# Scores of the HGRN2 layer on four quarters of the array, with the samples' products beside them

## The chip, the core and the metric

The kernel runs on one core of a Trainium2 chip. A core has five engines that matter here, each with its own instruction stream: TensorE (PE; the profile shows its weight loads apart, as PEld), VectorE (DVE), ScalarE (ACT), GpSimd (POOL) and SyncE (SP), whose queue here issues all transfers. Matrix products land in PSUM, a memory of eight banks with 128 partitions; a bank holds 512 F32 values of each partition. The metric is the time of one execution on the device in microseconds, lower is better.

## The reference, cut to what matters

One step of a two-layer decoder trunk: 256 new prompt tokens and 8 single-token samples go through a Conformer convolution layer, a feed-forward layer with a causal convolution, an HGRN2 layer (gated linear recurrence, 16 heads of 128 x 128 state) and a second feed-forward layer. The change touches only the HGRN2 layer. Its core, for one head:

```python
def step(S, inp):
    qc, kc, vc, gc = inp
    G = jnp.cumsum(gc, axis=1)
    o_inter = jnp.einsum('bthk,bhkv->bthv', qc * jnp.exp(G), S)
    rel = jnp.where(mask[None, :, :, None, None], G[:, :, None] - G[:, None, :], -jnp.inf)
    decay = jnp.exp(rel)
    A = jnp.einsum('bthk,btshk,bshk->bths', qc, decay, kc)
    o_intra = jnp.einsum('bths,bshv->bthv', A, vc)
    ...
```

So the output of token t is a sum over the earlier tokens s of a score, which is the product of query t and key s in each of 128 channels, weighted by the decay between the two tokens in that channel, times the value of s. The samples are single tokens with a state of their own: their state decays, takes in the outer product of key and value, and is multiplied by the query.

## The kernel before, in words

All activations stay on the chip, with channels on the partitions and the 264 tokens (256 and 8) along the free axis. Weights are streamed in tiles of 128 output channels. `slot` (L183) does one such tile: 16 steps over the input channels, each of three products of 264 columns in a fast F32 form (L179 to L181, a high and a low part of weight and activation), so 48 products of a slot. The parts are made ahead by ACT (`split_hi`, L137) and DVE (`split_lo`, L149).

PE, ACT and DVE run in the order in which the program is written. `later(k, fn)` (L159) puts a step into the turn of the slot that comes k + 1 slots later; within a turn (`slot`, L196 to L204), after the slot's 48 products have been put on PE, come the steps marked `first`, the casts, the unmarked steps, the splits on DVE, and the steps marked `last`. SP's order is made by a planner, which follows the data and the buffers.

In the HGRN2 stage each head takes three slots: `hf` (forget gate), `hq` (query), `hi` (value). After the heads in `GATE_AFTER` (3, 4, 6, 7, 9, 10, 12, 13, 15) comes one slot `hg` (output gate) of an earlier head, and the seven remaining `hg` slots come at the end. The stage is followed by the output projection (`ho`), whose first tile is a plain F32 product (L176).

The scores are computed without exponents of long sums. `doubling` (L677) makes, for b = 1, 2, 4, ..., 128, pairs `R[b]` of queries and keys, already decayed to the border inside blocks of 2b tokens. The score of tokens t and s is right in that level b in which s lies in the first and t in the second half of the same block of 2b; for t = s it is the plain product. So each level gives a matrix of which a mask keeps a part, and the masked levels are summed. `scores` (L741) does that inside blocks of 64 tokens: for each of the seven entries of `LV` (0, 1, 2, 4, 8, 16, 32) and each of the four blocks of 64 there is one product of 64 x 64 (L750), two blocks on the lower and two on the upper half of the array's columns, into `pl`, two banks. Then come level 128 (L753, 128 x 128) and level 64 (L756, two products of 64 x 64, both on the lower half) into one bank `pa`, and two transposes that turn keys for the state (L759). All are plain F32. `flip` (L709) turns the values, just ahead of `scores` in the same turn.

`select` (L761), one turn later, copies the parts of `pa` out on ACT, multiplies `pl` with the mask (L769) and sums over the levels (L772) on DVE; `place` (L774) copies the result into `AT`, the matrix of weights, whose part above the blocks of 64 comes from level 64 (L766). `outputs` (L796) multiplies by the values.

For the samples, `decay` (L779) scales the state on ACT, `sample_state` (L788) adds the outer products on DVE and writes the state out (L794), and `sample_outputs` (L806) multiplies it with the queries: eight products with 32 columns of weights, four of them side by side on four quarters of the array's columns, into `pos` (L813). That is a step of its own at the end of a turn, two turns after `decay`. After the last head `sample_rows`, `sample_columns`, `sample_squares`, `sample_sum` and `sample_norm` (L872 to L895) normalise all samples at once, and `samples_gated` (L923) applies the gates.

Of the kernel before, what the change touches and what calls it, by code (L numbers as in the profile page):

```python
# [8 lines left out]
F32 = mybir.dt.float32  # L9
# [3 lines left out]
ALU = mybir.AluOpType  # L13
AX = mybir.AxisListType
# [3 lines left out]
P = 128  # L18
# [6 lines left out]
HEADS = 16  # L25
# [20 lines left out]
AHEAD = 2  # L46
LOADS = 4
TE = 17

GATE_AFTER = (3, 4, 6, 7, 9, 10, 12, 13, 15)  # L50
HGRN, _g = [], 0
# [9 lines left out]
def kernel(ctx: ExitStack, tc: tile.TileContext, a: dict):  # L61
# [4 lines left out]
    cp = ctx.enter_context(tc.tile_pool(name="cp", bufs=1))  # L66
    sp = ctx.enter_context(tc.tile_pool(name="sp", bufs=1))
    wp = ctx.enter_context(tc.tile_pool(name="wp", bufs=3))
    ps = ctx.enter_context(tc.tile_pool(name="ps", bufs=5, space=PSUM))

    def bank(name):
        return ps.tile([P, 512], F32, tag="pt", name=name)
# [541 lines left out]
    with ExitStack() as ph:  # L614
# [3 lines left out]
        rstd = st.y  # L618
        later(0, st.finish, last=True)

        mask = cst[:, P:].rearrange("p (o n) -> p o n", o=1).to_broadcast((P, 2, len(LV) * 64))
        AT = [h1.tile([P, 2, P], F32, tag=f"AT{i}", name=f"AT{i}") for i in range(2)]
        for t in AT:
            vec.memset(t[64:, :, :64], 0.0)
        gss = h1.tile([P, HEADS, NB], F32, tag="gss", name="gss")

        NG = P // 32
# [113 lines left out]
        def scores(h):  # L741
            d = heads[h]
            R, qk, K = d["R"], d["qk"], d["K"]
            pl = d["pl"] = ps.tile([P, 2, 512], F32, tag="pl", name=f"pl{h}", bufs=1)
            for l, b in enumerate(LV):
                for hf in range(2):
                    for i in range(2):
                        s = (2 * hf + i) * 64
                        key, query = (qk[:, 2, :], qk[:, 0, :]) if b == 0 else (R[b][:, 1, :], R[b][:, 0, :])
                        pe.matmul(pl[i * 64 : i * 64 + 64, hf, l * 64 : (l + 1) * 64], key[:, s : s + 64], query[:, s : s + 64],  # L750
                                  start=True, stop=True)
            pa = d["pa"] = bank(f"pa{h}")
            pe.matmul(pa[:, :P], R[128][:, 1, :P], R[128][:, 0, P:SEQ], start=True, stop=True)  # L753
            for hf in range(2):
                s = hf * P
                pe.matmul(pa[:64, P + hf * 64 : P + (hf + 1) * 64], R[64][:, 1, s : s + 64], R[64][:, 0, s + 64 : s + P],  # L756
                          start=True, stop=True)
            for i, k in enumerate((K, R[128][:, 1, P:SEQ])):
                pe.transpose(pa[:, (2 + i) * P : (3 + i) * P], k, ident)  # L759

        def select(h):  # L761
            d = heads[h]
            pa, pl, W = d.pop("pa"), d.pop("pl"), AT[h % 2]
            Kt = d["Kt"] = hp.tile([P, 2, P], F32, tag="Kt", name=f"Kt{h}", bufs=1)
            act.copy(Kt, pa[:, 2 * P :].rearrange("p (i k) -> p i k", i=2))
            act.copy(W[:64, :, 64:], pa[:64, P : 2 * P].rearrange("p (o t) -> p o t", o=2))  # L766
            A1 = d["A1"] = hp.tile([P, P], F32, tag="A1", name=f"A1_{h}", bufs=1)
            act.copy(A1, pa[:, :P])
            vec.tensor_tensor(out=pl[:, :, : len(LV) * 64], in0=pl[:, :, : len(LV) * 64], in1=mask, op=ALU.mult)  # L769
            lm = pl[:, :, : len(LV) * 64].rearrange("p o (l t) -> p o t l", t=64)  # L770
            wd = heads[h]["wd"] = hp.tile([P, 2, 64], F32, tag="wd", name=f"wd{h}", bufs=1)
            vec.tensor_reduce(out=wd, in_=lm, axis=AX.X, op=ALU.add)  # L772

        def place(h):  # L774
            for i in range(2):
                r = slice(i * 64, i * 64 + 64)
                act.copy(AT[h % 2][r, :, r], heads[h]["wd"][r])

        def decay(h):  # L779
            d = heads[h]  # L780
# [146 lines left out]
        for name, h in HGRN:  # L927
            pt, = slot([(name, h)], hl)
            if name == "hf":
                later(0, lambda h=h, pt=pt: forget(h, pt), first=h > 0)  # L930
            elif name == "hq":
                if h == 0:
                    later(0, turned, last=True)
                    later(1, windows, last=True)
                later(0, lambda h=h, pt=pt: query(h, pt), first=True)
                later(0, lambda h=h: doubling(h, 1, 4), last=True)
            elif name == "hi":
                later(0, lambda h=h, pt=pt: value(h, pt), first=True)
                later(0, lambda h=h: doubling(h, 4, SEQ))
                later(1, lambda h=h: flip(h), last=True)  # L940
                later(1, lambda h=h: scores(h), last=True)
                later(2, lambda h=h: rows(h), first=True)
                later(2, lambda h=h: select(h))
                later(2, lambda h=h: place(h), last=True)
                later(3, lambda h=h: decay(h))
                later(3, lambda h=h: outputs(h), last=True)
                later(4, lambda h=h: squares(h), first=True)
                later(4, lambda h=h: sample_state_and_norm(h))
                later(5, lambda h=h: sample_outputs(h), last=True)
                later(5, lambda h=h: normed(h))  # L950
                later(6, lambda h=h: flop(h), last=True)
                later(7, lambda h=h: columns(h), first=True)
                if h == HEADS - 1:
                    later(6, sample_rows, first=True)
                    later(6, sample_columns, last=True)
                    later(7, sample_squares, first=True)
                    later(7, sample_sum, last=True)
                    later(8, sample_norm, first=True)
                    later(8, lambda: samples_gated(0, HEADS - 2), last=True)
                    later(8, lambda: samples_gated(HEADS - 2, HEADS), last=True)  # L960
            else:
                later(0, lambda h=h, pt=pt: gates(h, pt), first=True)
                later(0, lambda h=h: gated(h))
# [15 lines left out]
    with ExitStack() as ph:  # L979
        yp = ph.enter_context(tc.tile_pool(name="yp", bufs=1))  # L980
        Q = D // 4
        y = [yp.tile([P, D], F32, tag=f"y{i}", name=f"y{i}") for i in range(2)]
        ys = yp.tile([P, KT, NB], F32, tag="ys", name="ys")
        turned = {}

        def turn_back(i, c, pt):
            turned[i, c] = pt
            for j in range(4):
                pe.transpose(pt[:, j * P : (j + 1) * P], x[4 * c + j][:, i * P : (i + 1) * P], ident)

        pl = ps.tile([P, 2, 512], F32, tag="pl", name="p_y", bufs=1)
        pt = ps.tile([P, 512], F32, tag="st", name="p_ss", bufs=1)
        for i in range(2):
            turn_back(i, 0, bank(f"p_y{i}_0"))

        for i in range(3):
            for src, first in (st.acc, True), (st.last, False):
                if i < 2:
                    pe.matmul(pt[:, i * P : i * P + 1], src[:, i * P : (i + 1) * P], ones[:, :1], start=first, stop=not first)
                else:  # L1000
                    pe.matmul(pt[:, SEQ:T], ones, src[:, SEQ:], start=first, stop=not first)
        for i in range(2):
            turn_back(i, 1, pl[:, i, :])
        steps, r = [], []
        for s, w in (pt[:, 0:SEQ:P], 2), (pt[:, SEQ:T], NB):
            v, t, z = (yp.tile([P, w], F32, tag=f"{name}{w}", name=f"final_{name}{w}") for name in "vtr")
            vec.tensor_scalar(out=v, in0=s, scalar1=1.0 / D, scalar2=EPS, op0=ALU.mult, op1=ALU.add)
            steps.append(rsqrt_steps(z, v, t))
            r.append(z)
        for _ in zip(*steps):  # L1010
            pass
        for c in range(2, 4):
            for i in range(2):
                turn_back(i, c, bank(f"p_y{i}_{c}"))
        for c in range(4):
            d = slice(c * Q, (c + 1) * Q)
            act.activation(y[0][:, d], turned[0, c], AF.Identity, scale=r[0][:, 0:1])
            vec.tensor_scalar(out=y[1][:, d], in0=turned[1, c], scalar1=r[0][:, 1:2], scalar2=None, op0=ALU.mult)
            if c == 1:
                vec.tensor_tensor(out=ys, in0=xall[:, :, SEQ:], in1=r[1].unsqueeze(1).to_broadcast((P, KT, NB)), op=ALU.mult)  # L1020
                nc.sync.dma_start(a["o_ys"], ys)
            for i in range(2):
                nc.sync.dma_start(a["o_y"][i * P : (i + 1) * P, d], y[i][:, d])
# [93 lines left out]
```

## Time and profile before

| what | us |
|---|---|
| median of three runs (2478.6 to 2479.64) | 2479.0 |
| the profiled execution | 2478.74 |
| its span, first to last instruction | 2477.0 |
| PE busy over the span | 2446.4 |
| DVE busy over the span | 1759.9 |
| ACT busy over the span | 1110.7 |
| HGRN2 stage with its end, from 1132 to 1594 | 462 |
| in it, busy: PE, DVE, ACT | 455.4, 371.6, 267.1 |

The first two lines are times of whole executions; everything below comes from the profile of one of them, so a sum made from the profile is set against 2478.74. An engine is busy while it has an instruction in work. Products are pipelined, so PE's busy time alone doesn't say how well the array is used; starts of successive products do. The granted clock of PE was 0.996 of full speed over the span.

### The profile page before, as it was taken

To read this page: it belongs to the slowest core of one execution; us is meant where nothing else is said; L and a number is where in the kernel's file an instruction comes from. 1 tells how busy PE (TensorE), PEld (TensorE's weight loads), DVE (VectorE), ACT (ScalarE), POOL (GpSimd) and SP (SyncE) were. 2 spreads that over 40 slices of the span, in tenths; PEclk is the share of its full clock that TensorE was granted. 3 is DMA by queue.
4 is the path that set the end of the run, shared out by engine and by line. 5 is a ranking of instruction groups with operands and counts; after the bars stand their busy time and mean duration, and the time that the engine had idled before them with its cause. 6 is when DMAs were issued, how large, how long until landed. Compare 5 with 4: busy or idle time off the path is not lost.

```text
span 2477.0 us, 46795 instructions
## 1 busy us (share of the span) xinstructions
PE 2446.4 (99%) x19878; PEld 2391.7 (97%) x19878; DVE 1759.9 (71%) x3087; ACT 1110.7 (45%) x1759; POOL 0.2 (0%) x4
## 2 busy tenths in 40 slices
PE   8999899999999999999999999899999999999998
PEld 7888899999999999999999999899999999999998
DVE  8999867766566567568887888657767657656655
ACT  1112645444344344345655665444444444435434
POOL 0000000000000000000000000000000000000000
PEclk9999999999999999999999999999999999999999
DMA  7444445554554554555655655455555455455453
GB/s 270 150 153 142 169 173 204 176 182 156 202 187 161 182 196 164 180 182 197 232 190 202 222 208 199 161 182 199 176 187 173 158 205 180 158 201 186 164 176 129
DMA packets 78129, 452.92 MB, mean 183 GB/s; under 512 B 8544, under 2 KB 13024, under 8 KB 39008
## 3 DMA queue, kind: packets, MB, share of 16 engines
q1 hardware_dynamic: 77920, 449.94, 51.6%
q8 instruction: 155, 2.54, 0.4%
q14 instruction: 54, 0.44, 0.0%
HBM read 436.31 MB, written 15.50 MB: 182 GB/s over the span
## 4 chain that ended last, share of the span: by engine, by line
PE 99%; DVE 1%; issue 0%; DMA 0%; ACT 0%; ACTq 0%; SPq 0%; DVEq 0%
PE p_up L181 14%; PE p_up L179 14%; PE p_up L180 14%; PE p_pw L176 10%; PE p_dn L181 7%; PE p_dn L180 7%; PE p_dn L179 7%; PE p_hi L179 1%; PE p_hg L179 1%; PE p_hf L179 1%; PE p_hq L179 1%; PE p_hf L181 1%; PE p_hg L181 1%; PE p_hq L181 1%; PE p_hi L181 1%; PE p_hi L180 1%
## 5 line engine op out<-in xcount | busy, mean ns | idle before, releaser
L179 PE MATMUL p_up<-h_ffn,wh_up 128*128 128x264 f32 x2816 | 801.1, 284 | 0.0
L181 PE MATMUL p_up<-h_ffn,wl_up 128*128 128x264 f32 x2816 | 800.7, 284 | 0.0
L180 PE MATMUL p_up<-l_ffn,wh_up 128*128 128x264 f32 x2816 | 797.5, 283 | 0.0
L149 DVE TENSOR_TENSOR wl_up<-w_up,wh_up 128x2048 fp32r<-128x2048 f32 x176 | 403.5, 2293 | 231.9 <-ACT wh_up L137 231.9
L137 ACT CAST wh_up<-w_up 128x2048 fp32r<-128x2048 f32 x176 | 335.9, 1909 | 505.9 <-PE p_up L180 446.8
L179 PEld LDWEIGHTS p_up<-h_ffn,wh_up 128*128 128x128 f32 x2816 | 530.1, 188 | 0.1
L181 PEld LDWEIGHTS p_up<-h_ffn,wl_up 128*128 128x128 f32 x2816 | 530.0, 188 | 0.0
L180 PEld LDWEIGHTS p_up<-l_ffn,wh_up 128*128 128x128 f32 x2816 | 529.6, 188 | 0.1
L181 PE MATMUL p_dn<-gh,wl_dn 128*128 128x264 f32 x1408 | 400.8, 285 | 0.0
L179 PE MATMUL p_dn<-gh,wh_dn 128*128 128x264 f32 x1408 | 400.3, 284 | 0.0
L180 PE MATMUL p_dn<-gl,wh_dn 128*128 128x264 f32 x1408 | 400.1, 284 | 0.0
L137 ACT CAST wh_dn<-w_dn 128x1408 fp32r<-128x1408 f32 x128 | 175.9, 1374 | 325.9 <-PE p_dn L180 243.8
L149 DVE TENSOR_TENSOR wl_dn<-w_dn,wh_dn 128x1408 fp32r<-128x1408 f32 x128 | 208.1, 1626 | 108.3 <-ACT wh_dn L137 108.3
L180 PEld LDWEIGHTS p_dn<-gl,wh_dn 128*128 128x128 f32 x1408 | 265.3, 188 | 0.0
L181 PEld LDWEIGHTS p_dn<-gh,wl_dn 128*128 128x128 f32 x1408 | 264.7, 188 | 0.0
L179 PEld LDWEIGHTS p_dn<-gh,wh_dn 128*128 128x128 f32 x1408 | 264.6, 188 | 0.0
L176 PE MATMUL p_pw<-xg,w_pw 128*128 128x264 f32 x960 | 213.9, 386 | 0.0
L176 PEld LDWEIGHTS p_pw<-xg,w_pw 128*128 128x128 f32 x960 | 182.4, 190 | 31.2
L567 DVE SCALAR_TENSOR_TENSOR C<-H,par,C 128x255 f32<-128x255 f32 x352 | 169.1, 480 | 6.3
L278 DVE TENSOR_TENSOR x<-x,p_dn 128x264 f32<-128x264 f32 x128 | 54.9, 429 | 111.9 <-PE p_dn L181 111.9
L561 DVE TENSOR_TENSOR H<-p_up,rstd_ffn 128x264 f32<-128x264 f32 x176 | 76.1, 432 | 78.3 <-PE p_up L181 78.3
L562 ACT ACTIVATE C<-H,par 128x264 f32<-128x264 f32 x176 | 105.5, 600 | 13.9 <-DVE H L561 13.9
(316 smaller groups left out, 4007.9 us busy)
## 6 DMA issues: line engine op xcount, KB each, us to landing
w_up<-in_up SPq DMA_DIRECT2D x176, 1024.0 KB
w_dn<-in_dn SPq DMA_DIRECT2D x128, 704.0 KB
w_pw<-in_pw SPq DMA_DIRECT2D x47, 1024.0 KB
w_hf<-in_hf SPq DMA_DIRECT2D x16, 1024.0 KB
w_hq<-in_hq SPq DMA_DIRECT2D x16, 1024.0 KB
w_hi<-in_hi SPq DMA_DIRECT2D x16, 1024.0 KB
w_hg<-in_hg SPq DMA_DIRECT2D x16, 1024.0 KB
w_ho<-in_ho SPq DMA_DIRECT2D x16, 1024.0 KB
```

What stands on the lines that cost most here:

```text
L137: act.copy(wh[:, :kk, :], raw[key][:, :kk, :])
L149: vec.tensor_tensor(out=wl[:, :kk, :], in0=raw.pop(key)[:, :kk, :], in1=wh.bitcast(F32)[:, :kk, :], op=ALU.subtract)
L176: pe.matmul(pt[:, :T], wh[:, k, :], full[k], start=(k == 0), stop=last)
L179: pe.matmul(pt[:, :T], wh[:, k, :], rh, start=(k == 0), stop=False)
L180: pe.matmul(pt[:, :T], wh[:, k, :], rl, start=False, stop=False)
L181: pe.matmul(pt[:, :T], wl[:, k, :], rh, start=False, stop=last)
L278: vec.tensor_tensor(out=x[n], in0=x[n], in1=pt[:, :T], op=ALU.add)
L561: vec.tensor_tensor(out=h, in0=pt[:, :T], in1=rstd, op=ALU.mult)
L562: act.activation(cc, h, AF.Identity, scale=wv[:, j, 2:3], bias=pcol("ffn_b", layer * 2 * FT + j))
L567: vec.scalar_tensor_tensor(out=cc[:, d:SEQ], in0=h[:, : SEQ - d], scalar=wv[:, j, 2 - d : 3 - d], in1=cc[:, d:SEQ], op0=ALU.mult, op1=ALU.add)
```

## The change

`scores` works in blocks of 32 tokens. For the levels 0 to 16 each of the eight blocks of 32 is one product of 32 x 32, on the quarter of the array's columns that belongs to its place in the 128 tokens. Level 32 is no longer masked: of each block of 64 only the rectangle of the first 32 keys and the second 32 queries is computed. Level 64 is cut into four products of 32 keys by 64 queries, one on each quarter. All these, and then the sample products of the head before (`sample_outputs(h - 1)`), stand in a row ahead of level 128. `pl` is one bank instead of two, and the pool of general banks grows from five to six.

`select` masks and sums six levels of 32 columns instead of seven of 64 (384 values of each partition instead of 896). Level 32 is copied straight from `pl` into `AT` by two copies, level 64 by two instead of one, and `place` makes four copies instead of two. `AT` is cleared whole at the start of the stage, and the mask is rearranged by two copies there.

The sample products of a head are no step of their own any more, apart from those of the last head, which stand one turn earlier than before; the steps that normalise the samples all move one turn up, and `sample_norm` is no longer at the head of its turn. At the kernel's end one of the transposed parts of the output takes a general bank, since `pl` has only one.

```diff
+B = 32
+NL = len(LV) - 1
...
-    ps = ctx.enter_context(tc.tile_pool(name="ps", bufs=5, space=PSUM))
+    ps = ctx.enter_context(tc.tile_pool(name="ps", bufs=6, space=PSUM))
...
-        mask = cst[:, P:].rearrange("p (o n) -> p o n", o=1).to_broadcast((P, 2, len(LV) * 64))
+        by_level = cst[:, P:].rearrange("p (l t) -> p l t", t=64)
+        for r in (B, 3 * B):
+            act.copy(by_level[r : r + B, :NL, :B], by_level[r : r + B, :NL, B:])
+        mask = by_level[:, :NL, :B].unsqueeze(1).to_broadcast((P, 2, NL, B))
...
-            vec.memset(t[64:, :, :64], 0.0)
+            vec.memset(t, 0.0)
...
-            pl = d["pl"] = ps.tile([P, 2, 512], F32, tag="pl", name=f"pl{h}", bufs=1)
+            pl = d["pl"] = ps.tile([P, 2, len(LV), B], F32, tag="pl", name=f"pl{h}", bufs=1)
+            pa = d["pa"] = bank(f"pa{h}")
             for l, b in enumerate(LV):
+                key, query = (qk[:, 2, :], qk[:, 0, :]) if b == 0 else (R[b][:, 1, :], R[b][:, 0, :])
                 for hf in range(2):
-                    for i in range(2):
-                        s = (2 * hf + i) * 64
-                        key, query = (qk[:, 2, :], qk[:, 0, :]) if b == 0 else (R[b][:, 1, :], R[b][:, 0, :])
-                        pe.matmul(pl[i * 64 : i * 64 + 64, hf, l * 64 : (l + 1) * 64], key[:, s : s + 64], query[:, s : s + 64],
-                                  start=True, stop=True)
-            pa = d["pa"] = bank(f"pa{h}")
+                    for i in range(0, P // B, 1 if b < B else 2):
+                        s = hf * P + i * B
+                        t = s if b < B else s + B
+                        pe.matmul(pl[i * B : i * B + B, hf, l, :], key[:, s : s + B], query[:, t : t + B], start=True, stop=True)
+            for hf in range(2):
+                for i in range(2):
+                    r, s = 2 * hf + i, hf * P
+                    pe.matmul(pa[r * B : r * B + B, P : P + 64], R[64][:, 1, s + i * B : s + i * B + B],
+                              R[64][:, 0, s + 64 : s + P], start=True, stop=True)
+            if h > 0:
+                sample_outputs(h - 1)
             pe.matmul(pa[:, :P], R[128][:, 1, :P], R[128][:, 0, P:SEQ], start=True, stop=True)
-            for hf in range(2):
-                s = hf * P
-                pe.matmul(pa[:64, P + hf * 64 : P + (hf + 1) * 64], R[64][:, 1, s : s + 64], R[64][:, 0, s + 64 : s + P],
-                          start=True, stop=True)
...
-            act.copy(W[:64, :, 64:], pa[:64, P : 2 * P].rearrange("p (o t) -> p o t", o=2))
+            for hf in range(2):
+                act.copy(W[:64, hf, 64:], pa[hf * 64 : hf * 64 + 64, P : P + 64])
...
-            vec.tensor_tensor(out=pl[:, :, : len(LV) * 64], in0=pl[:, :, : len(LV) * 64], in1=mask, op=ALU.mult)
-            lm = pl[:, :, : len(LV) * 64].rearrange("p o (l t) -> p o t l", t=64)
-            wd = heads[h]["wd"] = hp.tile([P, 2, 64], F32, tag="wd", name=f"wd{h}", bufs=1)
-            vec.tensor_reduce(out=wd, in_=lm, axis=AX.X, op=ALU.add)
+            for r in range(0, P, 64):
+                act.copy(W[r : r + B, :, r + B : r + 64], pl[r : r + B, :, NL, :])
+            vec.tensor_tensor(out=pl[:, :, :NL, :], in0=pl[:, :, :NL, :], in1=mask, op=ALU.mult)
+            wd = heads[h]["wd"] = hp.tile([P, 2, B], F32, tag="wd", name=f"wd{h}", bufs=1)
+            vec.tensor_reduce(out=wd, in_=pl[:, :, :NL, :].rearrange("p o l t -> p o t l"), axis=AX.X, op=ALU.add)
...
-            for i in range(2):
-                r = slice(i * 64, i * 64 + 64)
-                act.copy(AT[h % 2][r, :, r], heads[h]["wd"][r])
+            for r in range(0, P, B):
+                act.copy(AT[h % 2][r : r + B, :, r : r + B], heads[h]["wd"][r : r + B])
...
-                later(5, lambda h=h: sample_outputs(h), last=True)
...
-                    later(6, sample_rows, first=True)
-                    later(6, sample_columns, last=True)
-                    later(7, sample_squares, first=True)
-                    later(7, sample_sum, last=True)
-                    later(8, sample_norm, first=True)
-                    later(8, lambda: samples_gated(0, HEADS - 2), last=True)
+                    later(4, lambda: sample_outputs(HEADS - 1), last=True)
+                    later(5, sample_rows, first=True)
+                    later(5, sample_columns, last=True)
+                    later(6, sample_squares, first=True)
+                    later(6, sample_sum, last=True)
+                    later(7, sample_norm)
+                    later(7, lambda: samples_gated(0, HEADS - 2), last=True)
                     later(8, lambda: samples_gated(HEADS - 2, HEADS), last=True)
```

More of the change, by code (lines that the diff above doesn't have):

```diff
@@ L989, in turn_back @@
                 pe.transpose(pt[:, j * P : (j + 1) * P], x[4 * c + j][:, i * P : (i + 1) * P], ident)
-        pl = ps.tile([P, 2, 512], F32, tag="pl", name="p_y", bufs=1)
+        pl = ps.tile([P, 512], F32, tag="pl", name="p_y", bufs=1)
         pt = ps.tile([P, 512], F32, tag="st", name="p_ss", bufs=1)
@@ L1002 @@
         for i in range(2):
-            turn_back(i, 1, pl[:, i, :])
+            turn_back(i, 1, bank(f"p_y{i}_1") if i else pl)
         steps, r = [], []
```

## The prediction

> **What bounds the kernel now.** First the page: engines, then the chain that ended last.
>
> ```profile
> PE 2446.4 (99%) x19878; PEld 2391.7 (97%) x19878; DVE 1759.9 (71%) x3087; ACT 1110.7 (45%) x1759; POOL 0.2 (0%) x4
> PE 99%; DVE 1%; issue 0%; DMA 0%; ACT 0%; ACTq 0%; SPq 0%; DVEq 0%
> ```
>
> TensorE carries the end, so a saved microsecond of TensorE in the HGRN2 stage is a microsecond of the kernel, as long as nobody else becomes late. Next the waits of PE in that stage (1132 to 1600), and the stretches of it (columns: length, then busy time of PE, PEld, DVE, ACT).
>
> ```profile
> PE p_ho L176 <- issue: 6.3, 1, 6.3
> PE p_sc L878 <- ACT sample_rows L874: 0.4, 1, 0.4
> 1443.00:1465.00 22.00, 22.00 (x224) 21.57 (x222) 19.43 (x45) 14.88 (x35) 0.00 (x0) 1.00 0.65 231
> 1588.00:1594.00 6.00, 0.01 (x1) 0.04 (x1) 5.04 (x19) 1.78 (x2) 0.00 (x0) 0.78 0.54 176
> ```
>
> PE waits twice in 460 us, both at the stage's end. In a three-slot head (1443 to 1465) DVE is busy 19.4 of 22.0 us and ACT 14.9: DVE is the next bound. Now the chain in order of time, through the second head's burst and the first sample products (start, us, what):
>
> ```profile
> 1178.29 0.22 PE pv L714 x2
> 1178.62 1.78 PE pl L750 x56
> 1180.40 0.42 PE pa L753 x2
> 1180.81 0.38 PE pa L756 x4
> 1181.19 0.37 PE pa L759 x2
> 1181.56 0.12 PE p_hi L179
> ...
> 1187.40 0.58 PE pos L813 x16
> 1187.98 0.32 PE p_hf L179
> ...
> 1253.46 0.37 PE pv L714 x2
> ```
>
> The last row is of a later burst, and is used below. 28 score products stand as x56: a plain F32 product is two records, each with its own weight load. A head costs 1.78 + 0.42 + 0.38 + 0.37 = 2.95 us, its sample products 0.58, and the next product 0.32 where its fellows take 0.12: 3.85 us, of which the last 0.20 is refill after the return to the whole array.
>
> To part array time from switches, the timeline (start, us from first start to last end, records):
>
> ```profile
> 1178.12 0.38 PE L714 MATMUL pv<-cst,v 128*128 128x128 f32 x2
> 1178.34 0.27 PE L715 MATMUL pv<-cst,v 128*8 128x128 f32 x1
> 1178.54 0.69 PE L750 MATMUL pl<-qk 128*64 128x64 f32 x16
> 1179.06 1.34 PE L750 MATMUL pl<-R 128*64 128x64 f32 x40
> ...
> 1187.33 0.65 PE L813 MATMUL pos<-sm,alone_acc 128*32 128x128 f32 x16
> ```
>
> A record's own length (0.27 us at 128 columns, 0.22 at 64) is latency; its price is the gap between starts. Whole array, 128 columns: 0.38 - 0.27 = 0.11. Two halves, 64 columns: (1.34 - 0.22)/39 = 0.0287 a start, so 0.0575 a round of two, and a half is held 0.0575. Four quarters, 128 columns: (0.65 - 0.27)/15 = 0.025 a start, a round of four in about 0.11. So quarters do run side by side, with the same 0.11 each. From 128 to 64 columns the hold falls by 0.0525; by that slope 32 columns hold a quarter 0.0575 - 0.026 = **0.031 us** (estimate).
>
> **The change, part by part.**
>
> *Scores.* Per head now 28 rounds of 0.0575 = 1.61, plus 0.17 of switching in the 1.78; then four records of level 64 on one half, 4 x 0.0575 = 0.23 of the 0.38. Afterwards: six levels x 8 products, 4 of level 32, 4 of level 64: 56 products, 112 records (now 60). In rounds: 24 of four quarters, 4 of two (level 32 uses quarters 0 and 2 alone), 28 x 0.031 = 0.87; for level 64, still 64 queries long, 2 x 0.0575 = 0.11. Together 0.98. Saved: 1.84 - 0.98 = 0.86.
>
> *Switches.* Today six: 0.17 into the halves, 0.20 (L753: 0.42 less 2 x 0.11), 0.15 (L756), 0.15 (L759: 0.37 against 0.22 for the two L714 products without a switch), 0.14 (samples: 0.58 less 4 x 0.11), 0.20 (refill): 1.01. Afterwards one in (0.17) and one out (0.20, at L753): 0.37. Saved: 0.64.
>
> Together 0.17 + 0.98 + 0.44 + 0.42 + 0.22 + 0.12 = 2.35 for 3.85: **1.50 us** in each of the heads 1 to 15, which take the samples of the head before; head 0 has none (2.95 to 1.79: 1.16); the last sample group stays alone. 15 x 1.50 + 1.16 = 23.7. After the eight four-slot heads the samples lie today ahead of the transposes of `flip` in the same burst, and the way out costs 0.37 - 0.22 = 0.15 instead of 0.20: less 0.4. **23.3 us.**
>
> The unknown in this is the start pace. No row shows quarters asked for every 0.031/4 = 0.008 us for long. How fast it can go for a moment:
>
> ```profile
> 1187.33 0.32 PE L813 MATMUL pos<-sm,alone_acc 128*32 128x128 f32 x4
> 1187.33 0.16 PEld L813 LDWEIGHTS pos<-sm,alone_acc 128*32 128x32 f32 x8
> ...
> L813 PEld LDWEIGHTS pos<-sm,alone_acc x128: 106/110/110, 1187.3 to 1554.7; 128*32 128x32 f32 x128
> L813 PE MATMUL pos<-sm,alone_acc x128: 272/273/298, 1187.3 to 1554.8; 128*32 128x128 f32 x128
> ...
> L750 PEldq EVENT_SEMAPHORE  x1: 51/51/51, 1156.6 to 1156.6; - x1
> L750 PEldq EVENT_SEMAPHORE  x1: 51/51/51, 1156.8 to 1156.8; - x1
> ```
>
> Four products start within 0.32 - 0.298 = 0.02 us (0.007 a start; 0.298 is the longest of one), and eight weight loads of 32 columns in 0.16 - 0.11 = 0.05: two whole rounds of loads, 0.03 a round. The last two rows bound supply: the sequencer ran two waits inside head 0's scores, which narrow windows place at 1156.64 and 1156.80, 0.16 us apart, the first lasting 0.051. Waits fall between levels, and a level is 16 instructions (8 loads, 8 products): 16 in 0.11 us or less, 0.0068 each. At that pace 224 instructions take 1.52 us, not 0.98: 16 x 0.54 = 8.7 us lost. The slow end is 0.0287 a start, what scores pay today: 112 x 0.0287 = 3.21. I take 0.98, nearest to the quarter's own rows.
>
> *Weighed against a page.* The Trainium skill, "TensorEngine Tiling (Array Packing)", section Instruction Overhead, says that each matmul has about 60 cycles of overhead, so that a small free dimension should not be cut for tiling; "TensorE: Matmul & The Clock Gate", section "Wait — 56ns, not 53.3ns?", puts the floor at about 25 ns from start to start. By that pace 112 records take 2.8 us a head, and the sum would be 16 x 1.82 = 29.1 us worse. The trace speaks against it as a floor across quarters (0.007 us between starts), though no long average here is below 0.025.
>
> *DVE and ACT.*
>
> ```profile
> L769 DVE TENSOR_TENSOR pl<-pl,cst 128x896 f32<-128x896 f32 x14 | 15.3, 1090 | 0.9 <-PE pl L750 0.9
> L772 DVE TENSOR_REDUCE wd<-pl 128x128 f32<-128x896 f32 x14 | 15.3, 1092 | 0.5
> L777 ACT COPY AT<-wd 64x128 f32<-64x128 f32 x28 | 8.4, 302 | 0.2
> L766 ACT COPY AT<-pa 64x128 f32<-64x128 f32 x14 | 3.7, 261 | 0.0
> L137 ACT CAST wh_hi<-w_hi 128x2048 fp32r<-128x2048 f32 x13 | 24.8, 1906 | 0.0
> ```
>
> Mask and sum go from 896 to 384 columns: 2.18 us to between 0.94 (by columns) and, say, 1.3: DVE loses about 1 us a head and PE 1.50; DVE's 2.6 us of room in 22 take the difference. ACT gains five small copies (one of L766's kind, two out of the score bank, two more in `place`) at 0.26 to 0.30: 1.4 us on 14.9 of 22. Hidden behind PE; if that cover went, the casts would be late next. The larger memset and the two mask copies come once, under the first slots' products: nothing.
>
> *Waits that move.* The samples of head h-1 now stand inside scores(h): behind them on PE wait the level 128 product, the transposes and the whole next slot. SP's load of the next state tile, which waits for these products, comes sooner in three-slot heads and some 2 us later in four-slot ones, with weight loads queued behind it; the casts show 0.0 idle for a late weight, so nothing. Memory banks stay eight (five, two and one become six, one and one).
>
> ```profile
> 1178.64 0.34 SPq L794 DMA_DIRECT2D o_hs<-sm  x1
> ...
> 1303.64 0.34 SPq L794 DMA_DIRECT2D o_hs<-sm  x1
> ...
> 1304.76 1.78 PE pl L750 x56
> ```
>
> SP issues L794 when DVE has finished a head's state. For head 0 that is 1178.64, 0.02 after its neighbour's scores began to count; the samples would be asked about 1.1 later. For head 5 (1303.64, its neighbour's scores from 1304.76) room is about 2.2. No wait, though the first is near.
>
> *The stage's end.* The last samples move a slot earlier, and the chain to `sample_norm` with them.
>
> ```profile
> 1585.29 2.29 DVE L149 TENSOR_TENSOR wl_ho<-w_ho,wh_ho 128x2048 fp32r<-128x2048 f32 x1 [0.78 <-ACT wh_ho L137]
> 1587.34 0.38 PE L886 MATMUL p_so<-sample_sq,ones 128*128 128x128 f32 x2
> 1587.76 0.29 DVE L891 TENSOR_SCALAR sample_two<-p_so 128x128 f32<-128x128 f32 x1 [0.18 <-PE p_so L886]
> ...
> 1591.54 0.39 DVE L894 TENSOR_TENSOR o<-p_sc,sample_two 128x128 f32<-128x128 f32 x1
> 1591.77 0.42 DVE L654 TENSOR_TENSOR zg<-p_hg,rstd_after 128x264 f32<-128x264 f32 x1
> ...
> 1593.99 4.30 PE L176 MATMUL p_ho<-o,w_ho 128*128 128x264 f32 x9 [6.27 <-issue]
> ```
>
> From p_so's sum PE stands 6.3 us: 4.1 of norm (1587.76 to 1591.9), 2.2 of the last gate. Moved up, norm runs beside the last slot (48 products of 0.12, 5.8 us), but shares DVE there with the split (2.3) and the end of a gate (2.2 less its first 0.42 and a sigmoid on ACT, some 1.2): 0.2 + 4.1 + 1.2 + 2.3 + 0.2 = 8.0, so DVE is 2.2 late and PE stands about 2.2 + 2.2 = 4.4. Saved 1.9, the 0.4 wait for sample_rows and 0.2 of p_so's hand-over: **2.5 us** (bounds: 0.4, that wait alone, and 6.3 - 2.2 + 0.4 = 4.5).
>
> **Sum.** 23.3 + 2.5 = 25.8. The profiled execution took 2478.74 us (span 2477.0 and 1.7 around it; the median of the runs is 2479.0, 0.3 more). 2478.74 - 25.8 = **2452.9 us**.
>
> **Rivals.**
> - *A start is priced per record, however narrow* (the slower side). What scores pay today, 0.0287, would be the price of a start and not half a hold: 3.21 against 0.98, 16 x 2.23 = 35.7 us, 2488.6. It decides from 0.023 a start (0.98 + 25.8/16 = 2.59, over 112). For it: no average below 0.025. Against: gaps of 0.007, and that holds explain 0.11, 0.0575 and both averages. At 0.025, today's average of the samples, 2.80 and 2482.0: no change by measurement. (The floor on the Trainium skill's page "TensorE: Matmul & The Clock Gate", above, would be this case.)
> - *Supply.* The queue runs dry in 224 instructions and the sequencer's pace sets the burst: 2461.6 at 0.0068. For: a burst doubles its instructions. Against: that bound is an upper one.
> - *The samples wait for DVE.* If the state is 1 us too late in the seven heads with three slots behind them (0, 1, 2, 5, 8, 11, 14): 7 us, 2459.9. Against: 1.1 to 2.2 us of room, and a lighter DVE.
> - *The quarters don't overlap*, so the change doesn't do what it says: 104 x 0.031 + 8 x 0.0575 = 3.68, 2496.1. The row of sixteen in 0.65 us all but excludes it; I count it with the first.
>
> **Chances.** Forecast (2447 to 2458) 0.68; supply 0.12; samples waiting 0.05; the price per record 0.15, of which about 0.08 near 0.025 (no change) and 0.07 above. A measurement tells about 0.2%, 5 us, from no change. Faster 0.85, same 0.08, slower 0.07. The range 2447 to 2468 holds the first three and leaves out the last and some tails.
>
> **What will show it.** Right: pl with x104 in the chain at about 1.0 us with its switch, pos right behind with no switch, some 0.44; no L813 group alone but the last; the wait before p_ho near 4 us; no other PE wait. Wrong: starts 0.025 or more apart in pl; starts that slow down after the first dozens of a burst (supply); PE waits before L813 released by DVE's sm; casts idle for weights, or DVE pressed in the three-slot heads.

## The result and the profile after

The changed kernel takes 2498.97 us (median of four runs, 2497.88 to 2499.7) against 2479.32 us for the kernel before: 1.0078 of its time, 95% interval 1.0061 to 1.0096. The prediction was 2452.9 us, with a range of 2447 to 2468. It is wrong by 46 us and in its sign: the change costs 20 us where 26 were to be gained. The profiled execution took 2499.46 us, its span is 2497.6.

First the page of the changed kernel, engines and the chain that ended last, as they were shown for before.

```profile
PE 2449.9 (98%) x20710; PEld 2386.7 (96%) x20710; DVE 1741.5 (70%) x3087; ACT 1125.3 (45%) x1841; POOL 0.2 (0%) x4
PE 87%; DVE 6%; ACT 4%; issue 2%; DMA 1%; DVEq 0%; SPq 0%; ACTq 0%
```

Before, PE carried 99% of the chain. Now DVE carries 6% and ACT 4%, although DVE is busy for *less* time than before (1741.5 us against 1759.9). So DVE has not become too slow; it is late. The largest waits of PE in the HGRN2 stage (total us, times, longest) say for what:

```profile
PE pos L823 <- DVE sm L802: 6.3, 4, 1.9
PE p_hi L183 <- DVE wl_hi L151: 6.1, 4, 1.5
PE p_hq L183 <- DVE wl_hq L151: 6.1, 4, 1.5
PE p_ho L178 <- DVE o L935: 1.6, 1, 1.6
```

Before there was one such wait of size, 6.3 us at `p_ho`. Now PE waits for the samples' state (`sm`) and for the low parts of the weights (`wl_hi`, `wl_hq`). Both are DVE's work. The chain in order of time through one burst (start, us, what) shows that the burst itself does what it was to do:

```profile
1225.42 0.22 PE pv L720 x2
...
1225.75 1.01 PE pl L758 x70
...
1226.79 0.14 PE pa L762 x7
1226.93 2.05 PE pos L823 x16
1228.98 0.42 PE pa L766 x2
```

The scores inside blocks and level 64 take 1.18 us together (1225.75 to 1226.93), where before they took 1.78 and 0.38. (The chain names 70 of the 104 records of L758 in this burst; the trace has all 104.) The sample products behind them take 2.05 us in place of 0.58. DVE's timeline at the same place says why (start, us, engine, line, operation, count):

```profile
1225.64 0.34 DVE L802 SCALAR_TENSOR_TENSOR sm<-vb,ks,sm 128x128 f32<-128x128 f32 x1
...
1228.18 0.34 DVE L802 SCALAR_TENSOR_TENSOR sm<-vb,ks,sm 128x128 f32<-128x128 f32 x1
```

The head's eight states are made while PE already asks for them, and the products go at DVE's pace: the last state starts at 1228.18, and the next work of PE starts at 1228.98.

What made DVE late is on the waits of DVE, in the same stage:

```profile
DVE pl L781 <- ACT AT L780: 72.9, 16, 5.7
DVE wl_hg L151 <- ACT wh_hg L139: 18.3, 7, 4.0
DVE wl_hf L151 <- ACT wh_hf L139: 13.8, 6, 4.0
DVE wl_hq L151 <- ACT wh_hq L139: 11.4, 5, 2.3
```

The first row is new. In each of the 16 heads the mask on `pl` (L781) stands still until ACT has made the two copies of level 32 out of `pl` (L780): 4.6 us on average. Before, the mask's group had 0.9 us of idle time in all, and that was for PE. Here is what DVE and then ACT did at one such place:

```profile
1208.90 0.42 DVE L660 TENSOR_TENSOR zq<-p_hq,rstd_after 128x264 f32<-128x264 f32 x1
1213.30 0.57 DVE L781 TENSOR_TENSOR pl<-pl,cst 128x384 f32<-128x384 f32 x1 [3.97 <-ACT AT L780]
```

```profile
1209.36 0.42 ACT L681 ACTIVATE qk<-zq 128x264 f32<-128x264 f32 x1 [1.95 <-DVE zq L660]
1209.69 1.90 ACT L139 CAST wh_hf<-w_hf 128x2048 fp32r<-128x2048 f32 x1
1211.49 0.61 ACT L855 ACTIVATE on<-po,rr 128x128 f32<-128x128 f32 x2
1211.99 0.37 ACT L774 COPY Kt<-pa 128x256 f32<-128x256 f32 x1
1212.25 0.43 ACT L776 COPY AT<-pa 64x64 f32<-64x64 f32 x2
1212.69 0.27 ACT L778 COPY A<-pa 128x128 f32<-128x128 f32 x1
1212.85 0.41 ACT L780 COPY AT<-pl 32x64 f32<-32x64 f32 x2
```

The two copies take 0.41 us together. But in ACT's order they stand behind a step that needs `zq` (L681), then behind a cast of 1.90 us and four more steps. DVE waits for that whole queue: it is free at 1209.3 and starts at 1213.30.

The mask (entries 0 to 5 of `pl`) and the copies (entry 6) have no value in common. They share the bank, on the same partitions. Before, ACT took its parts from `pa` alone and DVE worked in `pl` alone, so that no order between the two was needed. The Trainium skill, "PSUM — Partial Sum Buffer", section "PSUM bank collisions raise a hardware error", says that two engines may not be in the same bank and the same group of 32 partitions at once, whatever addresses they touch, and that the compiler's scheduler puts a dependency between them. The trace agrees: 16 heads, 16 waits. (Whether the bank itself decides, or that both were given the same tile of memory, no run tells apart.)

### The profile page after: what moved, and what is told of

It reads as the page before. It is cut to its first block, busy times and chain, and to the rows that moved or that the text cites. A ratio compares the mean times of both kernels' runs of the same rounds, so it can differ in the third digit from the quotient of the medians.

```text
span 2497.6 us, 48516 instructions
## 1 busy us (share of the span) xinstructions
PE 2449.9 (98%) x20710; PEld 2386.7 (96%) x20710; DVE 1741.5 (70%) x3087; ACT 1125.3 (45%) x1841; POOL 0.2 (0%) x4
## 4 chain that ended last, share of the span: by engine, by line
PE 87%; DVE 6%; ACT 4%; issue 2%; DMA 1%; DVEq 0%; SPq 0%; ACTq 0%
PE p_up L183 14%; PE p_up L181 14%; PE p_up L182 14%; PE p_pw L178 10%; PE p_dn L183 7%; PE p_dn L182 7%; PE p_dn L181 7%; DVE R L703 1%; PE p_ho L181 1%; PE p_ho L182 1%; PE p_ho L183 1%; PE p_pw L182 1%; PE p_pw L181 1%; PE p_pw L183 1%; PE pos L823 1%
```

## Where the 20 us come from

For this table each start of a PE product is charged with the time to PE's next start, and the sums are taken over the stage (from 1132.4 us to the first product of `p_ho`) by groups of lines. A wait of PE is so charged to the product in front of it. "Mask first" is an experiment below, in which the mask no longer waits; "best" is the experiment "The key's product on ACT".

| us of starts | before | after | mask first | best |
|---|---|---|---|---|
| scores with levels 64 and 128 and transposes | 44.3 | 35.5 | 25.1 | 25.4 |
| sample products | 9.2 | 24.9 | 17.1 | 9.2 |
| the slots' products | 373.9 | 395.9 | 377.0 | 377.3 |
| all else in the stage | 34.0 | 28.1 | 26.7 | 26.5 |
| the stage | 461.4 | 484.3 | 445.9 | 438.4 |
| `p_ho`'s first tile | 9.1 | 7.0 | 7.0 | 7.0 |

The difference of after to before, 22.9 - 2.1 = 20.8 us, is within 0.2 us that of the spans, 20.6. Against "mask first" the changed kernel loses 38.4 us: 18.9 in the slots' products, most of it in waits for low parts; 10.5 in the scores, most of it the time between the last score and a late sample product; 7.7 in the sample products; 1.3 elsewhere.

## The experiments: is it the wait of the mask?

**Theory A**: the mask's wait makes DVE late, and PE then waits for DVE in several places. **Theory B**: the samples in the burst are the cause, since they ask for the state too early. **Theory C**: the narrow products or the bank layout themselves cost time.

*Level 32 into the other bank.* Its four products go to a free part of `pa`, and ACT copies from there. Nothing else changes.

```diff
-                        pe.matmul(pl[i * B : i * B + B, hf, l, :], key[:, s : s + B], query[:, t : t + B], start=True, stop=True)
+                        out = pl[i * B : i * B + B, hf, l, :] if b < B else pa[i * B : i * B + B, P + 64 + hf * B : P + 64 + hf * B + B]
+                        pe.matmul(out, key[:, s : s + B], query[:, t : t + B], start=True, stop=True)
...
-                act.copy(W[r : r + B, :, r + B : r + 64], pl[r : r + B, :, NL, :])
+                act.copy(W[r : r + B, :, r + B : r + 64], pa[r : r + B, P + 64 : 2 * P].rearrange("p (o t) -> p o t", o=2))
```

> The changed kernel, but level 32 is written into 64 free columns of the bank pa and copied from there, so that VectorE's mask no longer waits for ScalarE's copies out of the score bank. Theory A (that wait, 72.9 us of VectorE's idle time in 16 heads, makes VectorE late, and TensorE's waits for it are what the forecast missed): about 2453 us, the forecast (2447 to 2460); the idle time before the mask falls from 72.9 us to a few, the samples' products from 24.9 us of starts to 16 x 0.44 = 7 to 10, waits of TensorE for weight splits gone. Rival B (the samples stand in the burst too early, whatever the mask does): the samples still wait, 2475 to 2499.

Measured: 2461.94 us, 0.9928 of before [0.9913, 0.9943]. The products, copies and their number are those of the changed kernel; 37.0 us are gone with the shared bank. That is 2 us above the range on record for theory A, and far from the 2475 of the rival.

*Mask first.* The copies stay in the shared bank but stand behind DVE's mask and sum, so that ACT waits for DVE and not DVE for ACT.

```diff
-            for r in range(0, P, 64):
-                act.copy(W[r : r + B, :, r + B : r + 64], pl[r : r + B, :, NL, :])
             vec.tensor_tensor(out=pl[:, :, :NL, :], in0=pl[:, :, :NL, :], in1=mask, op=ALU.mult)
             wd = heads[h]["wd"] = hp.tile([P, 2, B], F32, tag="wd", name=f"wd{h}", bufs=1)
             vec.tensor_reduce(out=wd, in_=pl[:, :, :NL, :].rearrange("p o l t -> p o t l"), axis=AX.X, op=ALU.add)
+            for r in range(0, P, 64):
+                act.copy(W[r : r + B, :, r + B : r + 64], pl[r : r + B, :, NL, :])
```

> The changed kernel with one thing moved: VectorE's mask and sum are written ahead of ScalarE's two copies out of the score bank, so that ScalarE waits for VectorE and not the other way. The products and their banks are those of the changed kernel. Theory A: as with level 32 in pa, 2453 (2447 to 2460). Rival B: 2475 to 2499. Rival C (level 32 in another bank would help for another reason, such as two engines at one bank): this one stays near 2499 while the other falls.

Measured: 2461.08 us, 0.9925 [0.9908, 0.9941], so the rival C of this expectation, which had 2499 here, falls. All the waits of PE that the view lists for the stage, then the largest of DVE. (A product that starts late, but when the one before it has hardly ended, leaves too little idle time to be listed; the sample products of four heads are late in that way, as shown below.)

```profile
PE p_ho L178 <- DVE o L935: 1.7, 1, 1.7
PE p_hg L183 <- DVE wl_hg L151: 1.0, 3, 0.3
```

```profile
DVE wl_hg L151 <- ACT wh_hg L139: 31.8, 13, 4.0
DVE wl_hf L151 <- ACT wh_hf L139: 30.7, 14, 4.0
DVE wl_hq L151 <- ACT wh_hq L139: 13.9, 7, 2.3
```

This answers a question that the forecast should have asked: why couldn't DVE's idle time take the wait? In these three rows DVE idles 76.4 us; in the changed kernel 43.5, and 72.9 more in front of the mask. So of 72.9 us only 33 came out of idle time that was there, and the other 40.0 made DVE later. The kernel lost 37.9 (2498.97 - 2461.08). DVE's idle time lay in front of splits that wait for ACT's casts; it is not a store that any wait may draw on.

*Samples as before.* The changed kernel, its mask's wait kept, with `sample_outputs` a step of its own and the old end of the stage.

```diff
-            if h > 0:
-                sample_outputs(h - 1)
...
+                later(5, lambda h=h: sample_outputs(h), last=True)
...
-                    later(4, lambda: sample_outputs(HEADS - 1), last=True)
-                    later(5, sample_rows, first=True)
...
+                    later(6, sample_rows, first=True)
```

> The changed kernel with the sample products back as a step of their own, one turn later, and the end of the stage as before; the mask still waits for ScalarE. Theory A: VectorE is late all the same, and TensorE waits for the weight splits instead of for the states: 2485 to 2505. Rival B (the samples' place is the fault): the scores' gain shows, 16 x (2.95 - 1.79) = 18.6 us, 2460.

Measured: 2503.09 us, 1.0094 [1.0079, 1.0109]. The samples no longer wait, and nothing is won. PE's waits have moved:

```profile
PE p_hq L183 <- DVE wl_hq L151: 7.9, 8, 1.5
...
PE po L811 <- ACT AT L785: 6.0, 4, 1.5
PE p_hi L183 <- DVE wl_hi L151: 5.9, 4, 1.5
```

That DVE is late is not seen at one tile alone. Take one consumer away and another of DVE's products is waited for (`AT` is ACT's copy of the sums that DVE makes). Theory B, which expected 2460, falls as the cause.

*The wait alone, in the kernel before.* Two copies of the same size, 32 partitions by 64, go from `pl` into a tile that nobody reads, ahead of the mask. Everything else is the kernel before, with its wide scores and separate samples.

```diff
             act.copy(A1, pa[:, :P])
+            held = hp.tile([P, 2, 32], F32, tag="held", name=f"held{h}", bufs=1)
+            for r in (0, 64):
+                act.copy(held[r : r + 32], pl[r : r + 32, :, 384:416])
             vec.tensor_tensor(out=pl[:, :, : len(LV) * 64], in0=pl[:, :, : len(LV) * 64], in1=mask, op=ALU.mult)
```

> The kernel before with only the wait added: two small copies of 32 x 64 out of the score bank on ScalarE, ahead of VectorE's mask, into a tile that nobody reads. Theory A: VectorE loses about 4 us in each head; where three slots make a head it has 2.6 us of room in 22 and runs over, where four do it has 7 in 29 and does not: some 1.5 to 2 us in each of seven heads and a little beside, 2485 to 2500. Rival B: the wait costs nothing by itself, 2479 within 0.2%.

Measured: 2516.6 us, 1.0149 [1.0134, 1.0164]: 37.0 us slower than the kernel before (2479.58 in these runs). DVE's largest wait, then PE's:

```profile
DVE pl L772 <- ACT held L771: 68.4, 16, 5.4
```

```profile
PE p_hi L179 <- DVE zf L654: 6.7, 4, 1.7
...
PE po L806 <- ACT AT L780: 5.7, 4, 1.5
PE p_hg L181 <- DVE wl_hg L149: 4.6, 6, 1.5
```

The size was more than the 2485 to 2500 that I had put on record, for the reason given above: I had counted DVE's other idle time as free to take the wait. DVE's idle time in front of the splits of `hg`, `hf` and `hq` fell only from 59.3 us before to 43.4, so 16 of the 68.4 us came out of it. The finding is plain all the same. The wait was added where there was none and cost 37.0 us; taken out of the changed kernel, in two ways, it gave back 37.0 and 37.9. Theory A holds, and theory C falls: without the wait, the narrow scores gain.

## The experiments: what is left after it

With the wait gone the kernel takes 2461 us, 8 more than predicted. In "mask first" the sample products still take 17.1 us of starts. They are on time in most heads (0.57 us a burst; 0.78 in head 0) and late in heads 5, 8, 11 and 14, which are, after the first three, the heads with no gate slot behind them (1.41, 2.88, 2.87 and 2.87 us). PE's timeline for head 8 (start, us from first start to last end):

```profile
1376.50 2.95 PE L823 MATMUL pos<-sm,alone_acc 128*32 128x128 f32 x16
```

*No sample in the burst, no wait.* Level 32 in `pa`, `sample_outputs` a step of its own, the old end: scores alone.

> Level 32 in pa (no wait of the mask), and the sample products back as a step of their own one turn later, with the end of the stage as before: the narrow scores alone. Theory A: the scores keep their gain (chain of pl, pa and transposes 1.8 us a head for 2.95, 16 x 1.16 = 18.6 us, so 2461 from 2479.6); no wait of TensorE for states. If narrow scores gave nothing by themselves: 2479.

Measured: 2467.45 us (five runs), 0.9948 [0.9936, 0.9961]. The expectation is missed: it is some 6 us slower. The largest waits of PE, in the profile of the fastest of the five runs (2465.18 us):

```profile
PE p_ho L178 <- DVE o L934: 6.2, 1, 6.2
PE p_hi L183 <- DVE wl_hi L151: 1.4, 2, 0.7
PE p_hq L183 <- DVE wl_hq L151: 1.0, 2, 0.6
```

PE has become faster by about 1.1 us a head, and the splits are now late by some tenths of a microsecond in a few heads. By the count of starts the slots' products take 378.3 us for 373.9 before, 4.4 us more, and the scores save 17.3 us of the 18.6 expected. DVE is the next bound, as its 19.4 of 22.0 us had said.

*The samples in the burst, but for the four late heads.* "Mask first", with heads 5, 8, 11 and 14 as a step of their own, as before.

```diff
+OWN = (5, 8, 11, 14)
...
-            if h > 0:
+            if h > 0 and h - 1 not in OWN:
                 sample_outputs(h - 1)
...
+                if h in OWN:
+                    later(5, lambda h=h: sample_outputs(h), last=True)
```

> As the kernel with the mask ahead of the copies (2461.1), but the sample products of heads 5, 8, 11 and 14 are a step of their own, one turn later; all others stay in the next head's burst. In that run these four groups took 1.41, 2.88, 2.87 and 2.87 us instead of 0.57, each product waiting for its state on VectorE. Theory A (these waits are the rest of what the forecast missed): 7.7 us less waits, 4 x 0.34 us more switches, 2454.8 (2453 to 2457). If the waits only hide another lateness of VectorE (the splits): 2459 to 2461.

Measured: 2458.83 us, 0.9917 [0.9903, 0.993]. The samples are back at 9.4 us of starts, 7.7 less than in "mask first"; the time fell by 2.3, so the second of the two expectations is the nearer one. The rest has gone into splits that now come too late, in heads 11 and 14 and in the heads right behind 8, 11 and 14:

```profile
PE p_hi L184 <- DVE wl_hi L152: 2.5, 3, 1.0
PE p_hq L184 <- DVE wl_hq L152: 1.8, 2, 0.9
```

*The state ahead of a split.* "Mask first", with the state's eight operations moved apart from the norm's, into the turn of the next head's value slot and behind its `doubling`.

```diff
+            if h < HEADS - 1:
+                for _ in head_norm(h):
+                    pass
+                return
             for _ in zip_longest(sample_state(h), head_norm(h)):
...
+                if h > 0:
+                    later(0, lambda h=h: [None for _ in sample_state(h - 1)])
```

> As the kernel with the mask ahead of the copies, all sample products in the burst, but VectorE updates a head's state right behind the next head's doubling, ahead of a weight split, and not beside the norm of the head. Theory A: states come some 2.5 us sooner, the four waits go, 2453 to 2455; the splits come 2 to 3 us later, and if they are the tighter thing, TensorE waits for them and the time stays at 2460 or above.

Measured: 2474.39 us (eleven runs), 0.9981 [0.9972, 0.999], so 13 us slower than the order it changes. Heads 5, 8, 11 and 14 are cured (0.57 us each), but the eight heads with a gate slot behind them, where the next value slot comes a slot later, now take 1.45 to 1.89 us, and PE waits for splits, 7.3 us in the two largest rows:

```profile
PE p_hq L183 <- DVE wl_hq L151: 3.7, 4, 0.9
PE p_hi L183 <- DVE wl_hi L151: 3.6, 4, 0.9
```

This one order did not help; that no order of DVE's work would is not shown by it.

If DVE bounds these heads, less work for DVE must give the rest. Two experiments, both on "but for the four late heads":

*The key's product on ACT.* `K`, one operation of DVE per head at the end of `doubling`, goes to ACT.

```diff
-                    vec.tensor_scalar(out=K, in0=R[b][:, 1, :b], scalar1=g[:, 1, 0, 0:1], scalar2=None, op0=ALU.mult)
+                    act.activation(K, R[b][:, 1, :b], AF.Identity, scale=g[:, 1, 0, 0:1])
```

> As the kernel with four sample groups as their own step (2458.8), but the product that makes K (0.29 us on VectorE, behind the doubling and ahead of a split) runs on ScalarE. Theory A (after the mask's wait is gone VectorE is the bound of the three-slot heads, and 5.3 us of TensorE's waits are for splits that it makes late): 0.29 us less in each of about three heads in a row that carry the lateness, 1 to 3 us less, 2456 to 2458. If ScalarE is as tight: no gain, 2458.8 or above.

Measured: 2453.73 us, 0.9898 [0.9883, 0.9912], better than expected. The waits of PE that are left:

```profile
PE p_ho L179 <- DVE o L936: 1.6, 1, 1.6
PE p_hg L184 <- DVE wl_hg L152: 0.7, 2, 0.3
PE p_hi L184 <- DVE wl_hi L152: 0.6, 1, 0.6
PE p_hq L184 <- DVE wl_hq L152: 0.3, 1, 0.3
```

This version computes everything and is 25.5 us faster than before and 45 faster than the changed kernel.

*A shorter norm.* Here the norm of the heads makes one refinement step of the inverse root instead of three; the other two are left out.

```diff
-    def rsqrt_steps(y, v, t):
+    def rsqrt_steps(y, v, t, times=3):
...
-            yield from rsqrt_steps(d["rr"], ss, tt)
+            yield from rsqrt_steps(d["rr"], ss, tt, times=1)
```

> As the kernel with four sample groups as their own step (2458.8), with six of the eleven small steps of each head's norm left out (one refinement of the inverse root for three), some 1 us of VectorE's time beside and behind the state updates in each head. Theory A (VectorE bounds the three-slot heads): the 5.3 us of waits for splits go, 2453 to 2455, the forecast's figure. If the splits wait for something else (ScalarE's casts, weights): 2458.8 within 1.

Measured: 2452.83 us, 0.9894 [0.9878, 0.9911]. No wait of PE for a split is listed any more, and two different reliefs of DVE give times within 1 us of each other. So what was left after the mask's wait was mainly DVE's load; that it gathers in the three-slot heads is read from where the late splits stood.

## The experiment: the stage's end

*The kernel before with only its end moved.* The last head's samples and all that follows them one turn earlier, as in the change.

```diff
-                later(5, lambda h=h: sample_outputs(h), last=True)
+                later(5 if h < HEADS - 1 else 4, lambda h=h: sample_outputs(h), last=True)
...
-                    later(8, sample_norm, first=True)
-                    later(8, lambda: samples_gated(0, HEADS - 2), last=True)
+                    later(7, sample_norm)
+                    later(7, lambda: samples_gated(0, HEADS - 2), last=True)
```

> The kernel before with only the end of the stage changed: the last sample products and the steps behind them one turn earlier, the norm behind the gate of its turn. By the prediction's sum: 2.5 us less (2477.1). By the waits of the run with the mask ahead of the copies, where TensorE stood 1.7 us at the output projection instead of 6.3 and 0.4 and the projection's first tile then ran 2 us faster: 6 to 7 us less (2473).

Measured: 2472.21 us (seven runs), 0.997 [0.9958, 0.9981]: 7.1 us, where the prediction had 2.5. What PE waits for, all of it:

```profile
PE p_ho L176 <- DVE o L925: 1.7, 1, 1.7
```

The prediction let `p_ho` wait for two things that DVE does late, the split and then the last gate, 2.2 us each, and so kept a wait of 4.4. In DVE's timeline of this kernel the order at the end is this:

```profile
1586.53 2.28 DVE L149 TENSOR_TENSOR wl_ho<-w_ho,wh_ho 128x2048 fp32r<-128x2048 f32 x1
1588.74 0.27 DVE L925 TENSOR_TENSOR o<-o,gss 128x112 f32<-128x112 f32 x1
1588.92 0.42 DVE L654 TENSOR_TENSOR zg<-p_hg,rstd_after 128x264 f32<-128x264 f32 x1
...
1590.78 0.17 DVE L925 TENSOR_TENSOR o<-o,gss 128x16 f32<-128x16 f32 x1
```

`p_ho` begins at 1589.1, behind the first of the two L925 (the gates of the first fourteen heads). The last gate, from 1588.92 on, is made while PE works on the other heads' part of the tile. So the wait is 1.7 and not 4.4.

The tile itself takes 7.0 us of starts instead of 9.1. That is not for the gates: in the kernel before both L925 were made ahead of `p_ho` (from 1593.62 and 1593.80; it begins at 1593.99). It is PE's granted clock, the third number from the right in these rows, the first of the kernel before and the second of this one:

```profile
1594.00:1598.00 4.00, 4.00 (x9) 3.15 (x10) 3.23 (x10) 4.00 (x13) 0.00 (x0) 0.50 0.00 0
1589.00:1593.00 4.00, 3.94 (x18) 3.39 (x19) 2.48 (x10) 3.62 (x7) 0.00 (x0) 1.00 0.70 262
```

Behind the stand of 6.3 us the first products of the tile start 0.44 us apart, at half the clock, and the later ones 0.22; behind the stand of 1.7 us they start 0.22 apart from the second on. The prediction's own row of 4.30 us for nine products had shown it. Together 2.7 + 2.1 = 4.8, which is the 4.6 that were missing and a little more.

## Why the prediction was wrong, point by point

**The step that failed** is the one on DVE and ACT. It counted the new copies as ACT's time ("Hidden behind PE"), which they are: ACT has room for them. It did not ask what is waited for *by others* at the place where they stand. Two of them read the bank in which DVE multiplies in place, so that DVE's next step came to hang on ACT's queue: a wait that the sum put at nothing, and that measured 4.6 us a head and 37.0 to 37.9 us of the kernel. What was on record sufficed to see it: DVE busy for 19.4 of 22.0 us, ACT's cast of 1.9 us, and the order of a turn, which puts the casts ahead of these copies. The step named "DVE is the next bound" and then added a wait to DVE without noticing.

**DVE's load** was right as far as it went: mask and sum fell from 2.18 us to 1.12, inside the 0.94 to 1.3 on record.

```profile
L781 DVE TENSOR_TENSOR pl<-pl,cst 128x384 f32<-128x384 f32 x16 | 9.1, 566 | 72.9 <-ACT AT L780 72.9
...
L783 DVE TENSOR_REDUCE wd<-pl 128x64 f32<-128x384 f32 x16 | 8.9, 557 | 0.5
```

Against the 17 us saved in it over 16 heads (16 x 1.06) stand 72.9 us of new idle time in front of it. But DVE's room was counted too freely: 1 us a head less for DVE and 1.1 to 1.5 less for PE leaves the splits late in three-slot heads, worth some 5 us after the repair (2458.83 to 2453.73).

**The scores** were right. 1664 records take 15.1 us of starts when nothing is late, and level 64 another 2.6: 1.11 us a head, forecast 0.17 + 0.98 = 1.15. Scores, level 128 and transposes save 44.3 - 25.1 = 19.2 us; forecast 16 x 1.16 = 18.6. So the rivals "a price per start", "supply" and "no overlap" fall.

**The samples in the burst** gain less than forecast even when they are on time. They were to save 0.34 us a head, 0.14 by the switch and 0.20 by the refill. They take 0.57 us in the burst, with the way out to the whole array; the level 128 products behind them then save 0.10 a head (6.7 to 5.2 us over 16). In the slots, 51 gaps of about 0.21 us are left of 66, at 0.12 for a product without: 0.09 each. So about 0.2 a head, which is some 2 us less than forecast over all heads. The 0.20 had been read off a row of the chain, which charges more to a product than its start's gap.

**"The samples wait for DVE"** was on the list with 7 us and a chance of 0.05. In the changed kernel this happens in all the seven heads that it named (0, 1, 2, 5, 8, 11, 14) and in no other burst, with groups of 2.16 to 3.10 us in place of 0.57: 15 us, and 6.3 more of waiting ahead of some. (The last head's group, which stands alone, takes 1.28.) Its argument against ("a lighter DVE") is what the mask's wait took away. With the wait gone, head 0 is nearly on time and heads 1 and 2 are, as the 1.1 us of room had said. Heads 5, 8, 11 and 14 aren't, though the prediction gave head 5 some 2.2 us of room: in "mask first" the last state of head 8 ends at 1378.98, and PE began on the first at 1376.50.

**The end** was right in kind and too small: 7.1 for 2.5. The wait kept was 1.7 and not 4.4, and the 2.1 us that the projection's first tile gains by the clock were not in the sum.

**The sum** comes out nearly as forecast in the best version, 2453.73 for 2452.9, but partly by luck: the end gives 4.6 more, and the bursts give 25.5 - 7.1 = 18.4 for 23.3. Of these 4.9, four heads' samples outside the burst and the smaller gain of the other eleven are about 3, and the waits for splits 1.6.

## What to carry to other kernels

Beside the time of an added instruction, write down which bank or buffer it touches and which other engine touches that next; then read the queue of the engine that must be first, since the second one waits for all of it and not for the 0.4 us of the copy. Where two engines must read one PSUM bank, let the busier one go first in program order, or give each its own bank: either was worth 37 us here with the same work. An engine's idle time is room only if it lies where the wait falls; idle time in front of work that waits for someone else can't be spent earlier. And look at what runs behind a long stand of PE: the end of this stage gained 2.1 us there that no wait showed.

## What the runs showed of the hardware that was not expected

Products of 32 by 32, in turn on four quarters of the array's columns, hold a mean of 0.0091 us from start to start over whole bursts of 104 records (15.1 us for 1664), and one burst of two halves at 64 columns had 0.0287. The Trainium skill, "TensorE: Matmul & The Clock Gate", section "Wait — 56ns, not 53.3ns?", gives a floor of about 25 ns from start to start. By that figure 104 records would take 2.6 us (an estimate), and the chain shows 1.01. Where products go to different quarters the floor doesn't hold here; for one quarter by itself no run of this case tells.

After a stand of 6.3 us PE's granted clock was 0.50 for some 4 us; after one of 1.7 us it was 1.00. The other runs fit: with 6.2 or 6.3 us of standing (the kernel before and three of the experiments) the projection's first tile took 8.4 to 9.8 us, with 1.6 or 1.7 us (all others) 7.0. How long a stand it takes, no run here tells.

The mask's wait cost 37 us in both kernels, though their bursts differ by 1.1 us a head. That the order of ACT and DVE, which they share, sets the cost, and not PE, is a guess: the waits themselves differ (72.9 and 68.4 us), and no run parts the two.
